# Moving cache copies, weight sums and a sigmoid inside one hybrid decoder layer

## The chip, the cores and the metric

The kernel runs on one core of a Trainium2 chip. TensorE (PE) multiplies matrices, VectorE (DVE), ScalarE (ACT) and GpSimd (POOL) work element by element, and SyncE (SP) and POOL issue the transfers. The metric is the device time of one execution in microseconds, the median over several runs.

## The reference

One layer for a prompt of 1024 rows and 32 sample rows (8 sequences of 4), model width 1024. All is float32.

```python
xn = RMSNorm_pre(x); h = xn @ w_in     # columns: q_attn | k_attn | v_attn | q_ret | k_ret | v_ret |
                                       #   ret_gate | merge_gate_attn | merge_gate_ret
# branch A: sliding-window (128) attention with sinks, 8 query heads, 2 key/value heads
# branch B: retention, 4 heads, key 128, value 256, in chunks of 128:
scores = einsum('bihd,bjhd->bhij', q, k) * dmask
out    = einsum('bhij,bjhe->bihe', scores, v) + cross ; state = g**L * state + k_decayed^T v
# each branch projected to 1024, merged by per-channel sigmoid gates, then w_o
x = x + RMSNorm_post(mixer)
x = x + RMSNorm_post(ConvFFN(RMSNorm_pre(x)))   # u = xn @ w_up, conv of width 3, gelu(a) * b, @ w_down
# also returned: the last 128 keys and values of the prompt, the caches of the samples
# (old rows shifted by 4, new rows behind), the retention states and the convolution states
```

What matters here: the sample caches are the old caches from row 4 on, copied as they are; the merge multiplies each branch by the sigmoid of its gate columns; and `w_down`'s product follows the feed-forward's middle.

## The kernel before

**Products.** Each float32 operand is split into two parts of reduced precision, `hi` (a cast on ACT, L228, L243, L246, L331) and `lo` (the difference, on DVE, L223). A product is three matmuls: `hi` with `xh`, `hi` with `xl`, `lo` with `xh` (L255, L256, L257, function `mm3`). The large products also use a scheme with seven products in place of eight (`A11`, `A12`, `A22`, `S1` to `S4`). The S products need sums of quarters of the weights. For `w_r` (the retention branch's projection) and `w_down` a "quad" of four quarters is loaded on SP (`quad_load`, two transfers of 256 KB, L289), four DVE operations on 128x256 make the sums (`quad_sums`, L223), and one store of 512 KB on POOL's queue puts them into DRAM (`r_d`, `s_d`, L300), from where the later stage loads them as weights (`quad_weights`, L316).

**Stages.** Normalisation and attention come first. Then `stream` runs the input projection of the retention and gate columns in pairs of 128 columns, and each pair's post function (`post_qk`, `post_gate`, `post_ga`, `post_gm`) stores it to DRAM: `qk_d`, `gr_d`, `a_d`, `gm_d`. The generator is advanced by `adv(n)`, so that its matmuls fill PE between the steps of the sample's and the prompt's retention. Of the prompt's retention, block `g` has three steps: `front` (scores, L1132), `middle` (output and state, L1152) and `tail` (gating). Tile `tt` of a head is one block of 128 rows. The `tail` of the first blocks of each head also issues one quad each: two of `w_r` and one of `w_down`, in tiles `zt`, which have three buffers and also serve `post_ga` (L849) and `z_sums`. After the retention comes the merge: the `w_r` product in the order of `PORD`, with `z_done` adding each product into `Gr`, and `merge`, which loads the gate `g_in` and the gated attention branch `a_in`, applies the sigmoid on ACT (L1257), and multiplies and adds on POOL for the first four column tiles (L1260, L1261) and on DVE for the others. `w_o` is loaded and split in the same loop (`weights`, L234). Raw weights of both, `w_raw`, share two buffers. Then follow the product with `w_o` (L1343), the feed-forward (24 pairs, each with `w_up` weights, convolution, gelu, and from `down_sums` one quad of `w_down`), and the down projection.

**Order.** The code's order is not the engines' order. A scheduler with a timeline of its own orders the instructions of each engine by their dependences. Instructions that are pinned keep their order among each other; the quads' loads and the cache copies are pinned. `ld` issues on SP's queue, `st` on POOL's, and each queue is in order: an issue that waits for a buffer holds all behind it.

Of the kernel before, what the change touches and what calls it, by code (L numbers as in the profile page):

```python
# [9 lines left out]
F32 = mybir.dt.float32  # L10
F32R = mybir.dt.float32r
U32 = mybir.dt.uint32
AF = mybir.ActivationFunctionType
# [5 lines left out]
P = 128  # L19
# [4 lines left out]
DB, DS = 8, 4  # L24
# [86 lines left out]
HW = T // 4  # L111
# [9 lines left out]
def trunk(ctx, tc, I, O):  # L121
    nc = tc.nc
    mult, add, sub = ALU.mult, ALU.add, ALU.subtract
    V, S, G, TE = nc.vector, nc.scalar, nc.gpsimd, nc.tensor
    ld, st = nc.sync, nc.gpsimd

    def pool(name, bufs=1, stack=None, side="right", **kw):
        if stack is not None:
            kw.update(side=side, reuse_waits="tile")
        return (stack or ctx).enter_context(tc.tile_pool(name=name, bufs=bufs, **kw))  # L130

    w_in, w_up, w_down = I["w_in"][0], I["w_up"][0], I["w_down"][0]
    w_o, w_a, w_r = I["w_o"][0], I["w_a_proj"][0], I["w_r_proj"][0]
# [8 lines left out]
    r_d = dram.tile([4, 1, P, KD, 2 * P], F32, name="r_d")  # L142
# [9 lines left out]
    s_d = dram.tile([4, 3, P, KD, 2 * P], F32, name="s_d")  # L152
# [21 lines left out]
    rt_stack, ph_stack, sm_stack = (ExitStack() for _ in range(3))  # L174
# [5 lines left out]
    def pin(ins):  # L180
        tc.keep_in_program_order(ins)
# [110 lines left out]
    def quad_sums(d, m, pt, kk, q, eng=None):  # L292
        eng = eng or V
        q = q[:, :, :2 * P]
        a11, a12, a21, a22 = (q[:, r::2, u * P:u * P + P] for u in range(2) for r in range(2))
        ew(eng, a22, a21, a22, add)
        ew(eng, a21, a11, a21, sub)
        ew(eng, a11, a22, a11, sub)
        ew(eng, a12, a12, a11, sub)
        st.dma_start(out=d[m, pt, :, 4 * kk:4 * kk + 4], in_=q)  # L300

    def down_sums(n, q):
        quad_load(w_down, n // 6, n // 2 % 3, n % 2, q)
        quad_sums(s_d, n // 6, n // 2 % 3, n % 2, q)
# [337 lines left out]
    for v in range(2):  # L642
        a, b = halves[v], halves[1 - v]
# [129 lines left out]
    def quarters(t):  # L773
        return t.rearrange("p (k x) -> p k x", k=4)
# [35 lines left out]
    def ST(name, shape, dt=F32, **kw):  # L810
        return rp.tile(list(shape), dt, name=name, **kw)

    def of_half(d, j):
        return d.rearrange("i p t -> p i t")[:, :, 2 * HW * j:2 * HW * (j + 1)]

    def both(t):
        return t.rearrange("p (i c) -> p i c", i=2)
# [34 lines left out]

    def post_gm(m):
        def post(j, o):
            st.dma_start(out=of_half(gm_d[KD + m:KD + m + 2], j), in_=both(o))
        return lambda j, o: lambda: post(j, o)

# [213 lines left out]
        for _ in sample(h):  # L1071
            adv(3)

    for nm in "kv":
        pin(st.dma_start(out=O[nm + "_sample"][0].rearrange("b r k d -> b r (k d)")[:, 0:P - DS, :],
                         in_=I["cache_" + nm][0].rearrange("b r k d -> b r (k d)")[:, DS:P, :]))

    ph_stack.close()
    wx["raw"] = rp = pool("rp", 1, stack=ph_stack)

# [18 lines left out]
    zlast, gts, qks, vts, state, quads, NBLK = [], {}, {}, {}, {}, {}, 4 * NB  # L1099
# [60 lines left out]
    def tail(g, pt, o):  # L1160
        h, tt = divmod(g, NB)
        tr_ = turn(pt, o)
        a = NS + P * tt
        while a < NS + P * tt + P:
            j = a // (2 * HW)
            b = min(NS + P * tt + P, 2 * HW * (j + 1))
            z = both(gts[h, j])[:, :, a - 2 * HW * j:b - 2 * HW * j]
            V.tensor_tensor(out=z, in0=tr_[:, :, a - NS - P * tt:b - NS - P * tt], in1=z, op=mult)
            a = b
        if tt == 0:  # L1170
            g_ = both(gts[h, 0])[:, :, 0:NS]
            V.tensor_tensor(out=g_, in0=g_, in1=z8[:, h], op=mult)
        QS = [(w_r, r_d, h, 0, 0), (w_r, r_d, h, 0, 1), (w_down, s_d, 3, (20 + h) // 2 % 3, h % 2)]
        if tt < 3:
            quads[h, tt] = quarters(ST("zt", (P, T), bufs=3))
            w, _, *at = QS[tt]
            quad_load(w, *at, quads[h, tt])
        if 0 < tt < 4:
            quad_sums(*QS[tt - 1][1:], quads.pop((h, tt - 1)))
        if tt in (4, NB - 1):  # L1180
            z_sums(h, gts[h, tt // 5], tt // 5)

# [36 lines left out]
    for g in range(NBLK):  # L1219
# [4 lines left out]
        m = middle(g, *f)  # L1224
# [14 lines left out]
    ps_stack.close()  # L1239
    tr = pool("tr", 1, stack=tr_stack)  # L1240
    wop = pool("wop", 1, stack=ph_stack)
    gpool = pool("apool", 2, stack=ph_stack)
    p8 = ppool("p8", 4, ps_stack)
    Gr = [TT("Gr%d" % m) for m in range(KD)]

# [6 lines left out]
    def merge(m, half):  # L1252

        ga = [gpool.tile([P, 2, HW], F32, name=q) for q in ("g_in", "a_in")]
        for t, d in zip(ga, (gm_d[KD + m], a_d[m])):
            ld.dma_start(out=t, in_=halves_of(d)[:, :, half])
        S.activation(ga[0], ga[0], AF.Sigmoid)  # L1257
        v = halves_of(Gr[m])[:, :, half]
        eng = G if m < 4 else V
        eng.tensor_tensor(out=v, in0=v, in1=ga[0], op=mult)  # L1260
        eng.tensor_tensor(out=v, in0=v, in1=ga[1], op=add)  # L1261
# [31 lines left out]
    for pi, p in enumerate(PORD):  # L1293
        first = p not in (A12, S3, S4)
        for c in range(2):
            hi, lo = wnext
            if 2 * pi + c + 1 < 2 * len(PORD):
                wnext = z_weights(2 * pi + c + 1)
            for e in range(2):
                for j in range(2):  # L1300
                    if first:
                        zb[c, e, j] = ps_8(j)[:, :HW]
                    ps = zb[c, e, j]
                    zh, zl = z_place(2 * pi + j)
                    for k in range(4):
                        mm3(ps, hi[:, 4 * e + k], lo[:, 4 * e + k], zh[:, k], zl[:, k],
                            first and k == 0, k == 3, skip_group_check=not first)
                    z_done(p, 2 * c + e, j, ps)
        for n in {0: (8, 9), 1: (10, 11), 3: (12, 13)}.get(pi, ()):
            load_zt(n)  # L1310
        if p == A22:
            merged_to_X(0)
        for m in {0: (0,), 1: (1,), 2: (2,), 3: (3, 4), 4: (5,), 5: (6,), 6: (7,)}.get(pi, ()):
            wo.append(weights(1, D, [(lambda r: r[:, 0], w_o[m * P:(m + 1) * P, :])],
                              [wop, wop, tpool, tpool, tpool, tpool, tpool, None][m]))
    merged_to_X(1)
# [11 lines left out]
    for tt in [0, 4, SMP, 1, 2, 3, 5, 6, 7]:  # L1328
# [4 lines left out]
        o = TT("o_t", (P, D))[:r_]  # L1333
# [20 lines left out]
        r = rsqrt_mean(s2[:, 0:1], D, r_, 1)  # L1354
# [8 lines left out]
        r = rsqrt_mean(s1, D, r_, 1)  # L1363
# [78 lines left out]
    for p in (A11, S1, A12, S4):  # L1442
        r, half = {A11: (0, 0), A12: (1, 0), S1: (0, 1), S4: (1, 1)}[p]
# [92 lines left out]
    for i in range(len(plain), NPAIR):  # L1536
        if i == NPAIR - 1:
            conv(i - 1, *done)
        u = pair(i)
        if i < NPAIR - 1:  # L1540
            prepare(i + 1)
            conv(i - 1, *done)
        if i < NPAIR - 2:
            down_sums(i - 2, tr.tile([P, 4, HW], F32, name="t2"))
        done = u
    def down_weights(p, c, pt):

# [186 lines left out]
```

## Time and profile before

| | |
|---|---|
| median of 3 runs | 1677.59 us (1676.19 to 1682.43) |
| the profiled execution | 1682.11 us, its span 1680.3 us |
| PE busy | 1633.0 us, 97% |
| DVE, ACT, POOL busy | 1207.2, 862.6, 434.8 us |
| granted TensorE clock, mean | 0.992 |

The span runs from the first to the last recorded instruction; 1.8 us lie around it. The profiled execution is 4.5 us slower than the median. Times in the traces count from the span's start. The line of PE's busy tenths in 40 slices of 42 us shows where PE had gaps:

```profile
PE   8999999999998999989999999999999999999997
```

A digit 9 stands for 90% or more. The slices below 9 are the first, the last, and two in between, from about 504 and 714 us on.

### The profile page before, as it was taken

What the parts mean: (1) busy time and instruction counts of PE and PEld (TensorE: products, weight loads), DVE (VectorE), ACT (ScalarE), POOL (GpSimd) and SP (SyncE); (2) the same over time, 40 slices, a digit from 0 to 9 for tenths busy, and PEclk for the clock granted to TensorE, in tenths of its full rate; (3) what the DMA queues carried; (4) which work ended last, traced back from release to release, by engine and by line L of the source; (5) the groups of instructions that cost most, each with busy time, mean ns of one, the idle gap of its engine ahead of it and who ended that gap; (6) DMA issues with size and microseconds to landing.
All of it is one profiled execution on the core that took longest, in us unless ns stands there. A gap on an engine that the chain in (4) does not pass through costs nothing.

```text
span 1680.3 us, 32489 instructions
## 1 busy us (share of the span) xinstructions
PE 1633.0 (97%) x12551; PEld 1593.2 (95%) x12551; DVE 1207.2 (72%) x2035; ACT 862.6 (51%) x1890; POOL 434.8 (26%) x654
## 2 busy tenths in 40 slices
PE   8999999999998999989999999999999999999997
PEld 7999989899998999989788999999999999999997
DVE  7887737688465566558757988888888888455476
ACT  6565634466564644454433655555555556443343
POOL 4242420012243333241312122222222223111111
PEclk9999999999999999999999999999999999999998
DMA  7212222565777686487722144444444447866664
GB/s 199 67 46 74 75 71 104 178 214 194 228 249 222 203 254 205 159 278 227 221 95 87 47 157 154 157 154 146 146 146 146 152 154 252 253 185 201 192 185 148
DMA packets 275852, 278.22 MB, mean 166 GB/s; under 512 B 23552, under 2 KB 234784, under 8 KB 275681
## 3 DMA queue, kind: packets, MB, share of 16 engines
q1 hardware_dynamic: 241937, 159.58, 32.6%
q0 software_dynamic: 33760, 116.57, 19.9%
q8 instruction: 98, 1.61, 0.4%
q14 instruction: 57, 0.47, 0.1%
HBM read 184.24 MB, written 87.49 MB: 162 GB/s over the span
## 4 chain that ended last, share of the span: by engine, by line
PE 78%; DMA 8%; DVE 5%; issue 4%; ACT 2%; POOL 1%; SPq 1%; DVEq 0%; POOLq 0%; ACTq 0%
PE ps_m L255 9%; PE ps_m L257 9%; PE ps_m L256 9%; PE ps_t L256 7%; PE ps_t L255 7%; PE ps_t L257 7%; PE ps_q L255 4%; PE ps_q L257 4%; PE ps_q L256 4%; PE ps_mm L255 3%; PE ps_mm L256 3%; PE ps_mm L257 3%; DMA qk<-qk_d 1%; DMA w_raw<-in_w_o 1%; DMA w_raw<-in_w_in 1%
## 5 line engine op out<-in xcount | busy, mean ns | idle before, releaser
L255 PE MATMUL ps_q<-xh,w 128*128 128x264 f32 x512 | 153.7, 300 | 7.5 <-DVE pair L939 6.2
L223 DVE SCALAR_TENSOR_TENSOR w_lo<-w_raw,w_hi 128x1024 fp32r<-128x1024 f32 x83 | 103.2, 1249 | 73.1 <-ACT w_hi L228 61.1
L257 PE MATMUL ps_m<-xh,w_lo 128*128 128x264 f32 x512 | 146.4, 286 | 4.6 <-DVE w_lo L223 4.5
L255 PE MATMUL ps_t<-xh,w_hi 128*128 128x264 f32 (+2 forms) x524 | 149.5, 285 | 0.0
L256 PE MATMUL ps_t<-xl,w_hi 128*128 128x264 f32 (+2 forms) x524 | 149.2, 285 | 0.0
L257 PE MATMUL ps_t<-xh,w_lo 128*128 128x264 f32 (+2 forms) x524 | 148.5, 283 | 0.0
L256 PE MATMUL ps_q<-xl,w 128*128 128x264 f32 x512 | 147.7, 289 | 0.0
L255 PE MATMUL ps_m<-xh,w_hi 128*128 128x264 f32 x512 | 146.4, 286 | 0.0
L257 PE MATMUL ps_q<-xh,w 128*128 128x264 f32 x512 | 146.3, 287 | 0.0
L256 PE MATMUL ps_m<-xl,w_hi 128*128 128x264 f32 x512 | 146.0, 285 | 0.0
L223 DVE SCALAR_TENSOR_TENSOR w<-w_raw,w 128x512 fp32r<-128x512 f32 x152 | 103.7, 686 | 32.6 <-ACT w L331 31.4
L1484 DVE SCALAR_TENSOR_TENSOR c_out<-u_ext,fconst,c_out 128x1024 f32<-128x1024 f32 x96 | 121.9, 1281 | 2.6 <-ACT c_out L1480 0.5
L228 ACT CAST w_hi<-w_raw 128x1024 fp32r<-128x1024 f32 x62 | 65.2, 1052 | 103.8 <-PE ps_t L256 75.4
L331 ACT CAST w<-w_raw 128x512 fp32r<-128x512 f32 x152 | 94.0, 621 | 24.9 <-DVE w_raw L223 11.1
L255 PEld LDWEIGHTS ps_q<-xh,w 128*128 128x128 f32 x512 | 97.9, 191 | 9.0 <-DVE pair L939 6.9
L257 PEld LDWEIGHTS ps_m<-xh,w_lo 128*128 128x128 f32 x512 | 96.8, 189 | 5.3 <-DVE w_lo L223 5.3
L255 PEld LDWEIGHTS ps_t<-xh,w_hi 128*128 128x128 f32 x524 | 99.1, 189 | 0.1
L257 PEld LDWEIGHTS ps_t<-xh,w_lo 128*128 128x128 f32 x524 | 99.2, 189 | 0.0
L256 PEld LDWEIGHTS ps_t<-xl,w_hi 128*128 128x128 f32 x524 | 99.1, 189 | 0.0
L256 PEld LDWEIGHTS ps_q<-xl,w 128*128 128x128 f32 x512 | 97.9, 191 | 0.5
L257 PEld LDWEIGHTS ps_q<-xh,w 128*128 128x128 f32 x512 | 97.6, 191 | 0.1
L255 PEld LDWEIGHTS ps_m<-xh,w_hi 128*128 128x128 f32 x512 | 96.8, 189 | 0.0
(446 smaller groups left out, 6000.6 us busy)
## 6 DMA issues: line engine op xcount, KB each, us to landing
w_raw<-in_w_up SPq DMA_DIRECT2D x48, 512.0 KB, 4.3
w_raw<-in_w_in SPq DMA_DIRECT2D x42, 512.0 KB, 4.5
w_raw<-s_d SPq DMA_DIRECT2D x60, 256.0 KB, 4.2
t_d<-t POOLq DMA_DIRECT2D x24, 528.0 KB, 4.0
t<-t_d POOLq DMA_DIRECT2D x24, 528.0 KB, 4.9
t<-in_w_down SPq DMA_DIRECT2D x40, 256.0 KB, 4.5
s_d<-t POOLq DMA_DIRECT2D x20, 512.0 KB, 3.6
w_raw<-in_w_down SPq DMA_DIRECT2D x36, 256.0 KB, 4.9
```

Of the source, the lines that this page charges most:

```text
L223: pinned(V.scalar_tensor_tensor(out=out, in0=in0, scalar=1.0, in1=in1, op0=mult, op1=op))
L228: pinned(S.copy(out=hi, in_=src))
L255: TE.matmul(ps, wh, xh, start=start, stop=False, **kw)
L256: TE.matmul(ps, wh, xl, start=False, stop=False, **kw)
L257: TE.matmul(ps, wl, xh, start=False, stop=stop, **kw)
L331: S.copy(out=t[:, 0:4], in_=src)
L1484: V.scalar_tensor_tensor(out=c[:, NS:], in0=u[:, g, NU + t:NU + t + SEQ], scalar=sc[t], in1=c[:, NS:], op0=mult, op1=add)
```

## The change

Four edits:

1. The copies of the old cache rows to the outputs (496 KB each for keys and values, from DRAM to DRAM, issued on POOL's queue) are no longer between the sample's and the prompt's retention, pinned. They are written in the feed-forward's loop, at pairs 4 and 6, and not pinned.
2. The four quads of `w_down` of the retention's `tail` (numbers 20 to 23) move to the feed-forward's loop, at pairs 5, 9, 13 and 17, each behind that pair's own quad and through the same single buffer `t2`. The `w_r` quads are now at blocks 0 and 2 of a head.
3. The sigmoid of the merge gate leaves `merge` (16 operations on 128x528) for `post_gm` (8 on 128x1056), ahead of the store to `gm_d`.
4. `g_in` and `a_in` have three buffers each in place of two, and the `w_o` tiles 5, 6 and 7 are asked for at products 4, 4 and 5 in place of 4, 5 and 6.

```diff
@@ -852,6 +852,7 @@
 
     def post_gm(m):
         def post(j, o):
+            S.activation(o, o, AF.Sigmoid)
             st.dma_start(out=of_half(gm_d[KD + m:KD + m + 2], j), in_=both(o))
         return lambda j, o: lambda: post(j, o)
 
@@ -1071,10 +1072,6 @@
         for _ in sample(h):
             adv(3)
 
-    for nm in "kv":
-        pin(st.dma_start(out=O[nm + "_sample"][0].rearrange("b r k d -> b r (k d)")[:, 0:P - DS, :],
-                         in_=I["cache_" + nm][0].rearrange("b r k d -> b r (k d)")[:, DS:P, :]))
-
     ph_stack.close()
     wx["raw"] = rp = pool("rp", 1, stack=ph_stack)
 
@@ -1170,13 +1167,13 @@
         if tt == 0:
             g_ = both(gts[h, 0])[:, :, 0:NS]
             V.tensor_tensor(out=g_, in0=g_, in1=z8[:, h], op=mult)
-        QS = [(w_r, r_d, h, 0, 0), (w_r, r_d, h, 0, 1), (w_down, s_d, 3, (20 + h) // 2 % 3, h % 2)]
-        if tt < 3:
+        QS = [(w_r, r_d, h, 0, 0), (w_r, r_d, h, 0, 1)]
+        if tt in (0, 2):
             quads[h, tt] = quarters(ST("zt", (P, T), bufs=3))
-            w, _, *at = QS[tt]
+            w, _, *at = QS[tt // 2]
             quad_load(w, *at, quads[h, tt])
-        if 0 < tt < 4:
-            quad_sums(*QS[tt - 1][1:], quads.pop((h, tt - 1)))
+        if tt in (1, 3):
+            quad_sums(*QS[(tt - 1) // 2][1:], quads.pop((h, tt - 1)))
         if tt in (4, NB - 1):
             z_sums(h, gts[h, tt // 5], tt // 5)
 
@@ -1239,7 +1236,7 @@
     ps_stack.close()
     tr = pool("tr", 1, stack=tr_stack)
     wop = pool("wop", 1, stack=ph_stack)
-    gpool = pool("apool", 2, stack=ph_stack)
+    gpool = pool("apool", 3, stack=ph_stack)
     p8 = ppool("p8", 4, ps_stack)
     Gr = [TT("Gr%d" % m) for m in range(KD)]
 
@@ -1254,7 +1251,6 @@
         ga = [gpool.tile([P, 2, HW], F32, name=q) for q in ("g_in", "a_in")]
         for t, d in zip(ga, (gm_d[KD + m], a_d[m])):
             ld.dma_start(out=t, in_=halves_of(d)[:, :, half])
-        S.activation(ga[0], ga[0], AF.Sigmoid)
         v = halves_of(Gr[m])[:, :, half]
         eng = G if m < 4 else V
         eng.tensor_tensor(out=v, in0=v, in1=ga[0], op=mult)
@@ -1310,7 +1306,7 @@
             load_zt(n)
         if p == A22:
             merged_to_X(0)
-        for m in {0: (0,), 1: (1,), 2: (2,), 3: (3, 4), 4: (5,), 5: (6,), 6: (7,)}.get(pi, ()):
+        for m in {0: (0,), 1: (1,), 2: (2,), 3: (3, 4), 4: (5, 6), 5: (7,)}.get(pi, ()):
             wo.append(weights(1, D, [(lambda r: r[:, 0], w_o[m * P:(m + 1) * P, :])],
                               [wop, wop, tpool, tpool, tpool, tpool, tpool, None][m]))
     merged_to_X(1)
@@ -1540,8 +1536,14 @@
         if i < NPAIR - 1:
             prepare(i + 1)
             conv(i - 1, *done)
+        if i in (4, 6):
+            nm = "kv"[i // 2 - 2]
+            st.dma_start(out=O[nm + "_sample"][0].rearrange("b r k d -> b r (k d)")[:, 0:P - DS, :],
+                         in_=I["cache_" + nm][0].rearrange("b r k d -> b r (k d)")[:, DS:P, :])
         if i < NPAIR - 2:
             down_sums(i - 2, tr.tile([P, 4, HW], F32, name="t2"))
+        if i in (5, 9, 13, 17):
+            down_sums(20 + (i - 5) // 4, tr.tile([P, 4, HW], F32, name="t2"))
         done = u
     def down_weights(p, c, pt):
```

What this does to the order is shown at four places; names are tiles with their buffer's number, DMA rows have the form of one transfer.

POOL, where the prompt's retention starts, before: the copies, then the loads of the first v tiles (`vt`) and the masks.

```order
L1060 DMA out_ret_sample<-s0_5263 128x2x256
L995 TENSOR_TENSOR rs_5473<-ms_5471,mhalf_107 32x1
L1075 DMA out_k_sample<-in_cache_k 8x15872
L1075 DMA out_v_sample<-in_cache_v 8x15872
L1113 DMA vt_5493<-v_d_64 128x256
L1113 DMA vt_5495<-v_d_64 128x256
L1113 DMA vt_5497<-v_d_64 128x256
```

The same place after:

```order
L1061 DMA out_ret_sample<-s0_5263 128x2x256
L996 TENSOR_TENSOR rs_5473<-ms_5471,mhalf_107 32x1
L1110 DMA vt_5491<-v_d_64 128x256
L1110 DMA vt_5493<-v_d_64 128x256
L1110 DMA vt_5495<-v_d_64 128x256
L1114 DMA dm_5497<-in_dmask 128x128
```

The copies are gone from there. POOL at the program's start, before:

```order
masks.py:197 MEMSET ident_102 128x128
L214 MEMSET mhalf_107 128x16
L521 MEMSET qs8_134 128x256
masks.py:199 ISA
masks.py:199 AFFINE_SELECT ident_102<-ident_102 128x128
L585 MEMSET acos_147 128x1056
L586 MEMSET asin_148 128x1056
```

and after:

```order
masks.py:197 MEMSET ident_102 128x128
L214 MEMSET mhalf_107 128x16
L521 MEMSET qs8_134 128x256
L1541 DMA out_k_sample<-in_cache_k 8x15872
masks.py:199 ISA
masks.py:199 AFFINE_SELECT ident_102<-ident_102 128x128
L1541 DMA out_v_sample<-in_cache_v 8x15872
L585 MEMSET acos_147 128x1056
L586 MEMSET asin_148 128x1056
```

The copies now stand behind the first memsets, at the very start, and not among the feed-forward's instructions.

SP around the quads of the second head, before (`z` and `zt<-gm_d` are gates, `qk` retention tiles, `w_raw` the stream's weights):

```order
L289 DMA zt_6475<-in_w_r_proj 128x4x128 x2
L849 DMA zt_6525<-gm_d_57 128x2x528
L289 DMA zt_6574<-in_w_r_proj 128x4x128 x2
L873 DMA w_raw_6598<-in_w_in 128x8x128
L1106 DMA qk_6497<-qk_d_62 128x2x128
L1122 DMA z_6611<-gr_d_63 128x2x528
L289 DMA zt_6672<-in_w_down 128x4x128 x2
```

and after:

```order
L289 DMA zt_6465<-in_w_r_proj 128x4x128 x2
L849 DMA zt_6515<-gm_d_57 128x2x528
L874 DMA w_raw_6585<-in_w_in 128x8x128
L1103 DMA qk_6487<-qk_d_62 128x2x128
L1119 DMA z_6598<-gr_d_63 128x2x528
L289 DMA zt_6659<-in_w_r_proj 128x4x128 x2
L874 DMA w_raw_6823<-in_w_in 128x8x128
```

The `w_down` quad is gone and the second `w_r` quad stands three loads later, behind the next `w_raw`, a `qk` and a `z`.

SP in the merge, from the first S1 weights (`r_d`) on, before:

```order
L316 DMA w_raw_9545<-r_d_60 128x4x128 x2
L234 DMA w_raw_9654<-in_w_o 128x1024
L316 DMA w_raw_9660<-r_d_60 128x4x128 x2
L1256 DMA g_in_9580<-gm_d_57 128x2x264
L316 DMA w_raw_9737<-r_d_60 128x4x128 x2
L1256 DMA a_in_9581<-a_d_58 128x2x264
L1256 DMA g_in_9615<-gm_d_57 128x2x264
L234 DMA w_raw_9814<-in_w_o 128x1024
L1256 DMA a_in_9616<-a_d_58 128x2x264
L1256 DMA g_in_9695<-gm_d_57 128x2x264
L316 DMA w_raw_9820<-r_d_60 128x4x128 x2
```

and after:

```order
L316 DMA w_raw_9513<-r_d_60 128x4x128 x2
L234 DMA w_raw_9620<-in_w_o 128x1024
L1253 DMA g_in_9582<-gm_d_57 128x2x264
L1253 DMA g_in_9667<-gm_d_57 128x2x264
L234 DMA w_raw_9626<-in_w_o 128x1024
L1253 DMA a_in_9583<-a_d_58 128x2x264
L1253 DMA a_in_9668<-a_d_58 128x2x264
L316 DMA w_raw_9632<-r_d_60 128x4x128 x2
```

A second `w_o` load stands ahead of the second S1 tile (`w_raw_9632`). The end of that stretch after:

```order
L234 DMA w_raw_9782<-in_w_o 128x1024
L1253 DMA g_in_9853<-gm_d_57 128x2x264
L1253 DMA a_in_9854<-a_d_58 128x2x264
L1253 DMA g_in_9885<-gm_d_57 128x2x264
L1253 DMA a_in_9886<-a_d_58 128x2x264
L1253 DMA g_in_9917<-gm_d_57 128x2x264
L316 DMA w_raw_9788<-r_d_60 128x4x128 x2
L1253 DMA a_in_9918<-a_d_58 128x2x264
```

The second tile of S4 (`w_raw_9788`) now stands behind the gate load `g_in_9917`, where its counterpart `w_raw_9820` stood ahead of most of the last gates.

## The prediction

> **What bounds the kernel now.** I read the busy shares first, then the span cut by stage, then the waits of PE, and last the 40 us around each wait.
>
> ```profile
> PE 1633.0 (97%) x12551; PEld 1593.2 (95%) x12551; DVE 1207.2 (72%) x2035; ACT 862.6 (51%) x1890; POOL 434.8 (26%) x654
> 320.00:700.00 380.00, 366.66 (x2823) 358.84 (x2822) 243.57 (x498) 205.01 (x522) 116.43 (x182) 0.98 0.67 212
> 925.00:1410.00 485.00, 485.00 (x3993) 485.00 (x3992) 423.61 (x698) 279.78 (x573) 128.34 (x214) 1.00 0.45 146
> ```
>
> The first line is the page's; the others are stretches: length, then busy us of PE, weight loads, DVE, ACT and POOL, the granted clock, the DMA share and GB/s. PE is the bound: busy for 1633.0 us, and in the feed-forward stage (925 to 1410) for all of 485. No matmul is added or removed, so time can only come from PE's idle gaps and from slow clock, and both lie ahead of 840 us, in the projection and retention (320 to 700), the merge, and the start of the product with w_o behind it.
>
> ```profile
> PE ps_q L255 <- DVE pair L939: 6.2, 3, 5.0
> PE ps_m L257 <- DVE w_lo L223: 4.5, 2, 4.3
> PE ps_m L1343 <- DVE o_t L1357: 3.1, 1, 3.1
> PE ps_a L1132 <- DMA qk<-qk_d: 2.7, 1, 2.7
> 440.00:480.00 40.00, 37.26 (x265) 36.15 (x264) 17.94 (x39) 19.63 (x49) 10.99 (x19) 0.91 0.78 237
> 520.00:560.00 40.00, 35.02 (x253) 33.94 (x253) 23.81 (x55) 18.88 (x46) 13.76 (x22) 0.91 0.77 241
> 720.00:760.00 40.00, 35.68 (x280) 35.34 (x279) 25.18 (x19) 22.53 (x37) 18.66 (x16) 0.96 0.90 295
> 800.00:840.00 40.00, 36.95 (x197) 30.05 (x195) 28.19 (x48) 17.13 (x39) 16.30 (x13) 1.00 0.73 220
> ```
>
> The waits give the total, the count and the longest, in us. Each of the four longest lies alone in one of the stretches below it: qk in 440:480, the pair sum in 520:560, w_lo in 720:760, o_t in 800:840. A stretch with a granted clock of 0.91 lost another 40 x 0.09 = 3.6 us, the one at 0.96 lost 1.6, the last none. So the four places cost 2.7 + 3.6, 5.0 + 3.6, 4.3 + 1.6 and 3.1: 23.9 us, the most that this change can win there. Each edit touches one of them.
>
> **1. The cache copies.**
>
> ```profile
> 438.20 0.57 POOL L1075 DMA_DIRECT2D out_k_sample<-in_cache_k  x1
> out_v_sample<-in_cache_v POOLq DMA_DIRECT2D x1, 496.0 KB, 7.2
> 439.47 10.91 DMA qk<-qk_d
> w_raw<-in_w_in SPq DMA_DIRECT2D x42, 512.0 KB, 4.5
> qk<-qk_d SPq DMA_DIRECT2D x32, 128.0 KB, 3.7
> ```
>
> The timeline's and the chain's rows have start and duration, the DMA rows the size and the median time to landing. The first qk tile is issued on SP right behind a w_raw load, 1.3 us after the first copy, and lands 10.91 us later, where 3.7 is usual. A w_raw load usually takes 4.5; with qk behind it in the same queue I expect qk, without the copies, at 444 to 446 (439.47 plus 4.5, and up to 2 for its own bytes). PE stood from 447.7 to 450.4. In the changed order the first qk product stands behind 14 fewer matmuls, and at 37.26 / 265 = 0.14 us each it is asked for at about 445.7. So nearly all of 2.7 + 3.6 goes: -6.0 (ends -6.3 and 0, if w_raw and the v tiles held qk up, not the copies).
>
> The copies don't go where the code puts them. Nothing holds them to the feed-forward loop, and in the order of the changed kernel they stand on POOL at the very start, behind a handful of memsets. The feed-forward pays nothing, the start does:
>
> ```profile
> 0.92 0.31 POOL L521 MEMSET qs<- 128x256 f32 x1
> 3.14 1.05 ACT L490 ACTIVATE xn<-xt 32x1024 f32<-32x1024 f32 x1 [1.12 <-DMA xt<-in_x_sample]
> 3.28 3.75 PE L517 MATMUL ps_mm<-g_row,one 1*128 1x512 f32 x4 [3.28 <-DMA g_row<-in_g_pre_mix]
> 4.00:6.00 2.00, 2.00 (x4) 0.67 (x2) 0.72 (x2) 0.66 (x3) 0.54 (x1) 1.00 0.95 371
> 14.00:16.00 2.00, 1.42 (x4) 0.92 (x4) 2.00 (x4) 2.00 (x3) 0.00 (x0) 1.00 0.03 12
> ```
>
> Issued from 1.2 us on, behind that memset (0.92 + 0.31), they meet the first loads: PE and ACT wait for g_row and x until 3.2, and the DMA engines are full (0.95) just after, at 371 GB/s. At this rate 992 KB are 2.7 us. The loads that decide land by 3.3, when the copies have hardly begun, and by 14 the queue has run empty (0.03), which takes up the rest: I take +1.0, between 0 and 2.7 + 1.8 of slow clock. The issues (0.57 each) stand ahead of POOL's later work there and hide in its waiting.
>
> **2. The weight sums of the down projection.**
>
> ```profile
> 528.50 7.47 DMA r_d<-zt
> 536.46 6.25 DMA zt<-in_w_down
> 542.80 0.89 DVE L223 SCALAR_TENSOR_TENSOR zt<-zt 128x256 f32<-128x256 f32 x2 [6.93 <-DMA zt<-in_w_down]
> zt<-in_w_r_proj SPq DMA_DIRECT2D x16, 256.0 KB, 6.1
> ```
>
> Chain rows: the store of one quad frees its buffer at 535.97, the load of the w_down quad follows and lands at 542.71, and DVE stands 6.93 us before its sums, with the add that frees PE's bank behind them. With two quads a head the three buffers suffice and no load waits for a store. In the changed order the second w_r quad's load stands behind the next w_raw, a qk and a z; issued at about 530 and landing 6.1 later it is there at 536.1, where DVE arrives at 535.87 (542.80 less 6.93). I leave 1.0 of the 8.6: -7.6 (ends -8.6 and -3).
>
> What they cost in the feed-forward:
>
> ```profile
> L223 DVE SCALAR_TENSOR_TENSOR t<-t 128x256 f32<-128x256 f32 x80 | 33.5, 419 | 11.0 <-DMA t<-in_w_down 11.0
> 1040.00:1080.00 40.00, 40.00 (x331) 40.00 (x331) 33.45 (x57) 22.11 (x47) 9.13 (x16) 1.00 0.46 147
> t<-in_w_down SPq DMA_DIRECT2D x40, 256.0 KB, 4.5
> s_d<-t POOLq DMA_DIRECT2D x20, 512.0 KB, 3.6
> ```
>
> Four quads of four sums of 0.419 us are 6.7 us of DVE in 485, 1.7 us each time, and DVE has 6.5 idle us in 40. The 2 MB of loads and 2 MB of stores go over DMA engines that are 46% used. Cost 0; if the cover were gone, 6.7.
>
> **3. The sigmoid.**
>
> ```profile
> L1257 ACT ACTIVATE g_in<-g_in 128x528 f32<-128x528 f32 x16 | 10.2, 643 | 11.3 <-DMA g_in<-gm_d 10.9 <-DVE xl L223 0.3
> L843 ACT ACTIVATE pair<-pair 128x1056 f32<-128x1056 f32 x8 | 8.7, 1088 | 0.1
> 824.54 1.05 ACT L246 CAST w_hi<-w_raw 128x1024 fp32r<-128x1024 f32 x1 [7.55 <-DMA w_raw<-in_w_up]
> 825.49 0.64 ACT L1257 ACTIVATE g_in<-g_in 128x528 f32<-128x528 f32 x1
> 826.21 1.83 POOL L1260 TENSOR_TENSOR Gr<-Gr,g_in 128x528 f32<-128x528 f32 x1 [2.28 <-ACT g_in L1257]
> 830.58 0.60 ACT L1351 ACTIVATE o_t<-ps_m 128x512 f32<-128x512 f32 x1 [3.21 <-DVE xl L223]
> 739.07 1.23 DVE L223 SCALAR_TENSOR_TENSOR w_lo<-w_raw,w_hi 128x1024 fp32r<-128x1024 f32 x1 [0.55 <-ACT w_hi L228]
> 751.12 2.31 DVE L223 SCALAR_TENSOR_TENSOR w_lo<-w_raw,w_hi 128x1024 fp32r<-128x1024 f32 x1
> ```
>
> Sixteen of 0.643 go, eight of 1.088 (the like of L843's) come, where ACT is busy for 205 of 380 us: 0 to +2, taken +0.5 for bank evictions that stand behind them. At 824.5 the last sigmoid stands behind a cast that waited 7.55 us for a w_up tile; POOL's merge, DVE's split and ACT's o_t follow in that order, and PE waits 3.1. Without the sigmoid the merge waits for transfers and z products alone: -3.1 (ends -3.1 and 0). The 4.3 at w_lo are another thing: the same DVE form takes 2.31 us in place of 1.23 while POOL merges. The POOL work stays and only its times shift: -1.5 of 5.9 (ends -5.9 and +2).
>
> The Trainium skill's "SBUF — State Buffer", under "Who interferes with whom", says that a DVE operation with two SBUF inputs and a GpSimd operation that reads SBUF lock each other out for a whole instruction. The row of 2.31 agrees, and by this rule the 5.9 wouldn't fall at all.
>
> **4. Third buffer, w_o loads.** The raw weight tiles go round two buffers in SP's order. Before the second S1 tile there now stand two w_o loads where one stood, and the second S4 tile's load stands behind the last gates'.
>
> ```profile
> 779.12 3.67 DMA w_raw<-in_w_o
> 783.59 3.90 DMA w_raw<-r_d
> 788.68 0.66 DVE w_lo L223
> ```
>
> These are on the chain already, so there is no slack: one slot more is 783.59 - 779.12 = 4.5 us. In the changed order PE has w_o matmuls and the high products of several banks to do meanwhile. Taken +2.5, between 0 and 4.5 + 1.8 of slow clock.
>
> **Sum.** -6.0 + 1.0 - 7.6 + 0.5 - 3.1 - 1.5 + 2.5 = -14.2. The profiled execution took 1682.1 us, 4.5 over the median of 1677.6: so 1667.9. If that excess lies outside these places, the median comes to 1663.4; if it lies in them, to 1667.9. I take a third of it off: 1666, 11 to 12 us under the median of before.
>
> A rule would change the sum: "TensorE: Matmul & The Clock Gate" of the Trainium skill, under "What's actually happening", lets the clock fall after an idle window of about 3.4 us. By it the 2.7 us stall could cost no clock, and the sum would be 3.6 less: about 1670. The row of 0.91 at 440:480 says otherwise, the 1.00 after 3.1 idle us agrees, so I keep the row.
>
> **Rivals.** *New waits in the merge (0.15).* For it: term 4 lies on the chain, and a SP queue with more gate loads ahead of weights. Against: PE has other products in the order. At its end with a second such wait at S4, +7 instead of +2.5 and nothing won at w_lo: about 1672.
>
> *The start pays in full (0.12).* The copies hold g_row and x back: +4.5 for +1.0, about 1670, still inside the bound of 0.5%.
>
> *The DVE and POOL collision grows (0.08).* POOL's merges no longer wait for ACT, so they follow each other without a pause; w_lo operations double more often. +2 for -1.5, and half of the 3.1 stays: 1671. This is what the SBUF rule would make of it.
>
> *Slower (0.08): DVE stands in the feed-forward.* The added quads pass through one buffer: its store takes 3.6 us and the next load 4.5, so 8.1 from one quad's last sum to the other's first. Ten rows stand between them in DVE's order, at 33.45 / 57 = 0.59 us and 84% busy some 7 us. DVE would stand 1.1 us, which its 6.5 idle us cover; if the load comes late on SP's queue, 6 or more, with the adds that empty PE's banks behind it. From about 5 us on PE stops; four stops of 3.2 with 1.8 of slow clock are 20: 1686.
>
> **How the numbers follow.** The forecast has 0.57, with a range of its own of 1658 to 1669. About 0.5% (8.4 us) is what can be told from no change; faster means under 1669.2. The first three rivals end within it, but a few of their cases fall below: faster 0.60, same 0.32, slower 0.08. Low end: all of w_lo's 5.9, no new wait and the other two thirds of the 4.5: 1666 - 4.4 - 2.5 - 3.0 = 1656. High end: two of the rivals together, 1678.
>
> **What would show it.** qk landing before 447 and no PE wait at the first block of retention; two DMAs at 1 to 3 us on POOL, and the first PE instruction at 3.3 to 4.5; no DVE wait for zt over 2 us around 535; no PE wait for o_t after the merge; PE at 485 of 485 in the feed-forward. I am wrong if PE's waits for w_lo in the merge exceed 8 us together, if PE's start is later by over 3, or if the pair sum at 540 still waits for a zt load.

## The result, and the profile after

The changed kernel takes 1682.69 us (1677.58 to 1687.32), the kernel before 1676.32 us in the same comparison. The ratio is 1.0039, 95% interval 1.0028 to 1.0050: 6.5 us slower, where 10 to 12 us less were forecast. It is within the 0.5% that the prediction called no change, but clear of zero, on the other side, and above the 1678 that the prediction gave as its high end.

The profiled execution of the changed kernel took 1682.09 us, as much as the profiled one of the kernel before (1682.11). Against their medians the two stand differently: the one of before is 5.8 us above its median, the one of after is on it. So a second profile of the kernel before is needed beside the first; it comes below.

The page after, its busy times and PE's tenths:

```profile
PE 1633.1 (97%) x12551; PEld 1592.4 (95%) x12551; DVE 1207.4 (72%) x2035; ACT 863.2 (51%) x1882; POOL 428.8 (26%) x654
PE   7999999999999999999999999999999999999997
```

The two dents of before at 504 and 714 us are gone. The first slice has gone from 8 to 7. The waits of PE on which the reading rests (total, count, longest):

```profile
PE ps_a L461 <- DVE xn L494: 6.0, 2, 4.7
PE ps_b L1003 <- ACT o L997: 3.5, 2, 1.9
PE ps_a L1129 <- DVE state L1149: 3.3, 3, 2.3
PE ps_m L257 <- DVE w_lo L223: 2.8, 2, 2.2
PE ps_m L255 <- ACT u_ext L418: 2.0, 2, 1.3
PE ps_m L255 <- ACT w_hi L228: 1.6, 1, 1.6
PE ps_m L1339 <- DVE o_t L1353: 0.7, 1, 0.7
```

Lines stand a few lower than before. The waits for qk and for the pair sum at 540 are gone, the longest for w_lo is halved, o_t's is 0.7. In their place stand a wait of 4.7 at the start, longer waits for `state` and `o` (the retention's state and its output) than before, and new ones for `w_hi` in the merge and for `u_ext` (the feed-forward's products, as ACT writes them) in the feed-forward. By stretches, first before (the start), then after (the start and the feed-forward):

```profile
0.00:40.00 40.00, 33.55 (x190) 29.56 (x191) 28.87 (x54) 26.40 (x53) 16.39 (x29) 1.00 0.75 208
```

```profile
0.00:40.00 40.00, 28.67 (x159) 24.30 (x160) 27.06 (x45) 22.24 (x40) 16.03 (x28) 1.00 0.80 227
925.00:1410.00 485.00, 482.85 (x3969) 482.19 (x3969) 425.87 (x713) 277.67 (x571) 123.05 (x214) 1.00 0.48 153
```

PE does 4.9 us less in the first 40 us, and the feed-forward, full before, loses 2.2 us. The start after, in the timeline:

```profile
1.36 0.71 POOL L1541 DMA_DIRECT2D out_k_sample<-in_cache_k  x1
2.42 0.56 POOL L1541 DMA_DIRECT2D out_v_sample<-in_cache_v  x1
3.37 3.75 PE L517 MATMUL ps_mm<-g_row,one 1*128 1x512 f32 x4 [3.37 <-DMA g_row<-in_g_pre_mix]
10.17 1.06 ACT L490 ACTIVATE xn<-xt 128x1024 f32<-128x1024 f32 x1 [5.80 <-DMA xt<-in_x_prompt]
11.22 0.57 ACT L595 COPY g_pre<-ps_mm 128x512 f32<-128x512 f32 x1
12.20 2.74 PE L461 MATMUL ps_a<-ident,xn 32*128 32x32 f32 x12 [4.71 <-DVE xn L494]
```

and the two rows of it before:

```profile
5.63 1.06 ACT L490 ACTIVATE xn<-xt 128x1024 f32<-128x1024 f32 x1 [1.34 <-DMA xt<-in_x_prompt]
7.85 2.63 PE L461 MATMUL ps_a<-ident,xn 32*128 32x32 f32 x12 [0.45 <-DVE xn L494]
```

The copies are issued at 1.36 and 2.42 us, beside the first loads. The load that PE waits for first, g_row, is as early as before. The first prompt tile is not: ACT gets it at 10.17 in place of 5.63, its square is the first step to everything behind it, and PE stands from 7.5 to 12.2. The DMA engines were not full while it stood. The stretch from 8 to 9 us, first before, then after:

```profile
8.00:9.00 1.00, 0.97 (x7) 0.84 (x8) 1.00 (x2) 0.29 (x2) 0.00 (x0) 1.00 1.17 293
```

```profile
8.00:9.00 1.00, 0.00 (x0) 0.00 (x0) 0.00 (x0) 0.00 (x0) 0.00 (x0) 1.00 0.15 54
```

Their busy share (the last figure but one, summed from packet times) is 0.15 where it was 1.17. The tile is late, but not because the engines lacked bandwidth all that time; what held its data back is not shown.

### The profile page after: what moved, and what is told of

Same layout as the page of the kernel before. It is cut to its first block, busy times and chain, and to the rows that moved or that the text cites. A ratio compares the mean times of both kernels' runs of the same rounds, so it can differ in the third digit from the quotient of the medians.

```text
span 1680.3 us, 32499 instructions
## 1 busy us (share of the span) xinstructions
PE 1633.1 (97%) x12551; PEld 1592.4 (95%) x12551; DVE 1207.4 (72%) x2035; ACT 863.2 (51%) x1882; POOL 428.8 (26%) x654
## 4 chain that ended last, share of the span: by engine, by line
PE 75%; DMA 9%; DVE 9%; issue 3%; ACT 3%; SPq 1%; POOL 0%; DVEq 0%; ACTq 0%; POOLq 0%
PE ps_m L255 8%; PE ps_m L257 8%; PE ps_m L256 8%; PE ps_t L256 6%; PE ps_t L257 6%; PE ps_t L255 6%; PE ps_q L255 5%; PE ps_q L257 5%; PE ps_q L256 5%; PE ps_mm L255 2%; PE ps_mm L256 2%; PE ps_mm L257 2%; DMA zt<-in_w_r_proj 2%; DMA t<-in_w_down 2%; DMA w_raw<-in_w_o 1%
## 5 line engine op out<-in xcount | busy, mean ns | idle before, releaser
L255 PEld LDWEIGHTS ps_q<-xh,w 128*128 128x128 f32 x512 | 97.5, 190 | 3.1 <-ACT pair L917 1.5
L256 PEld LDWEIGHTS ps_m<-xl,w_hi 128*128 128x128 f32 x512 | 97.1, 190 | 0.1
```

The lines of the kernel that those rows point to most:

```text
L255: TE.matmul(ps, wh, xh, start=start, stop=False, **kw)
L256: TE.matmul(ps, wh, xl, start=False, stop=False, **kw)
```

## The experiments

Each is timed against the kernel before on the same chip; "ratio" is to that, with its 95% interval. Three dots in a diff stand for arguments that are the same.

**Where the copies stand.** Four kernels. `a_pin` is the changed kernel with the copies pinned in the feed-forward:

```diff
         if i in (4, 6):
             nm = "kv"[i // 2 - 2]
-            st.dma_start(...)
+            pin(st.dma_start(...))
```

> The changed kernel with its two cache copies pinned, so that POOL issues them in the feed-forward and not at the program's start. Theory 1 (the copies at the start are what the change lost): PE's wait of 4.7 us at 7.5 us and the later warm clock (23.1 for 19.8, 1.7 us) go, so some 6.4 us less than the changed kernel, 1676, and PE's shift against the kernel before is about 0 at 40 us. Rival (the other edits cost what they bring, and the start is made up by later slack): 1682, unchanged.

Measured: 1677.0 us, ratio 1.0002 (0.9994 to 1.0011). Six us less than the change, level with the kernel before. The copies' place makes the loss. The other edits, with the copies away from the retention, together bring nothing that can be told from zero.

`b_copy0` is the kernel before with the copies alone moved, not pinned:

```diff
-    for nm in "kv":
-        pin(st.dma_start(...))                # between the retentions
...
+        if i in (4, 6):
+            st.dma_start(...)                 # in the feed-forward's loop
```

> The kernel before with only the copies moved, unpinned as in the change, so that they stand at the program's start. Theory 1: +6.4 us at the start, and -6 where the first qk tile is no longer late: 1676 to 1677, the same as before. If the qk wait isn't the copies' doing, or a typical run of the kernel before doesn't have it: 1681 to 1683.

Measured: 1682.6 us, ratio 1.0045 (1.0032 to 1.0058). This edit alone is as slow as the whole change. The expected gain of 6 did not come. The time is in the range of the second case, but for neither of its reasons: the wait for qk is gone from this profile, and a second profile of the kernel before (below) has it.

`b_copyffn` is the same with `pin(...)` around the copies, so that POOL issues them in the feed-forward.

> The kernel before with only the copies moved, pinned in the feed-forward. Theory 1: the qk wait of 2.7 us and its slow clock of 3.4 go and nothing comes at the start: 1670. Rival (qk was late because of w_raw and the v tiles): the wait stays, 1676.

Measured: 1676.6 us, ratio 1.0003 (0.9993 to 1.0012). Both expectations missed: the qk wait is gone, and the time is the same. What PE waited for between 440 and 490 us, first in the kernel before (its second profile, below), then here:

```profile
PE ps_a L1133 <- DMA qk<-qk_d: 2.7, 1, 2.7
```

```profile
PE ps_a L1128 <- DVE state L1148: 1.5, 1, 1.5
PE ps_b L1002 <- ACT o L996: 1.4, 1, 1.4
```

2.7 us of waiting for a transfer became 2.9 us of waiting for the retention's own chain; that its DVE and ACT steps had run while PE waited for qk is the likely reason. This is not all of it: the clock of this stretch is better (1.00 in place of 0.96), and the table below shows that the kernel is ahead at 600 us and loses it again by 900.

`a_orig` is the changed kernel with the copies put back between the two retentions.

> The changed kernel with the copies put back to where the kernel before has them, the other edits kept. Theory 1: no start cost (-6.4), the qk wait is back (+6): about 1682, and what the other edits bring is to be read as this run less the kernel before. If the other edits bring the 14 us that the prediction's terms gave them less the new waits, 1670; if they bring nothing, 1676.

Measured: 1676.3 us, ratio 0.9999 (0.9989 to 1.0010). The other three edits together bring nothing that can be told from zero.

**A second profile of the kernel before** (`before2`, unchanged but for a comment line, so its lines stand one higher).

> The kernel before, unchanged, for a second profile of it. The first profiled execution took 1682.1 us, and the median of the runs is now 1676.2. If the four waits (qk 2.7, pair sum 5.0, w_lo 4.3, o_t 3.1, with 8.5 us of slow clock) belong to every execution, they stand here again with the same lengths, within 0.5 us, at a time near 1682. If the profiled execution had an unlucky clock, the waits are there and most of the 8.5 us of slow clock isn't: 1674 to 1678. If the waits themselves vary, two or more of the four are shorter by over 1 us.

Measured: 1675.5 us. Its waits, and the stretches with the granted clock (the last but two):

```profile
PE ps_m L258 <- DVE w_lo L224: 5.4, 2, 4.8
PE ps_q L256 <- DVE pair L940: 3.9, 2, 3.7
PE ps_m L1344 <- DVE o_t L1358: 0.6, 1, 0.6
```

```profile
440.00:480.00 40.00, 37.25 (x272) 36.01 (x271) 19.81 (x43) 19.99 (x51) 10.16 (x18) 0.96 0.85 258
520.00:560.00 40.00, 36.28 (x265) 34.95 (x263) 23.36 (x53) 19.17 (x48) 12.78 (x21) 0.96 0.76 238
720.00:760.00 40.00, 35.22 (x277) 35.00 (x276) 27.88 (x26) 24.12 (x42) 20.98 (x16) 0.96 0.89 281
```

The qk wait is the same to the tenth. The pair sum's is 3.7 in place of 5.0, o_t's 0.6 in place of 3.1, and the two stretches at 0.91 are at 0.96: 1.6 us of slow clock where the first profile had 3.6. So the four places hold 2.7 + 1.6, 3.7 + 1.6, 4.8 + 1.6 and 0.6: 16.6 us in this execution, 23.9 in the first.

With two profiles of the kernel before, progress can be compared. All traces have 12551 matmuls, so the table counts them: how much later (+) or earlier the matmul starts that this second profile starts at the given time. Each row is one execution.

| | 40 us | 300 us | 600 us | 900 us | 1450 us |
|---|---|---|---|---|---|
| the change | +5.0 | +6.1 | +2.5 | +3.7 | +6.6 |
| `b_copy0` | +4.1 | +5.2 | +5.2 | +10.8 | +10.8 |
| `b_k0` (next) | +1.7 | +2.8 | +4.5 | +3.5 | +3.5 |
| `b_copyffn` | +0.1 | +0.2 | -4.0 | -0.5 | -0.5 |
| `b_quads` (below) | -0.4 | -0.4 | -1.5 | -1.3 | -1.2 |

The change loses 5 us at the start, gains 3.6 between 300 and 600 us, and loses 1.2 up to 900 us and 2.8 in the feed-forward. `b_copyffn` is 4 us ahead at 600 us; waits between 610 and 840 us and the slow clock behind them take it back, and what makes these was not tried.

**How much copy at the start.** `b_k0` has the key copy at the start, the value copy pinned in the feed-forward.

```diff
+        if i == 4:
+            st.dma_start(... "k" ...)
+        if i == 6:
+            pin(st.dma_start(... "v" ...))
```

> The kernel before with the key copy alone at the program's start and the value copy pinned in the feed-forward. With both at the start the time was 6 us more than with both in the feed-forward. Theory 1 (the copies' bytes stand in the way of the first prompt tile's load, and ACT waits for that tile in its order, with the gate row's copy behind it): half the bytes, so x lands some 2.3 us late in place of 4.5, PE's wait grows by 2.3, and the time is 1678 to 1680. Rival (the first copy alone holds the engines until the tile is late, or it is a fixed cost of any copy there): 1682. Rival (the first copy hides and the second does the harm): 1676.

Measured: 1680.5 us, ratio 1.0025 (1.0014 to 1.0035), between the rivals, nearest to theory 1. The row that answers:

```profile
9.00 1.06 ACT L490 ACTIVATE xn<-xt 128x1024 f32<-128x1024 f32 x1 [2.47 <-DMA xt<-in_x_prompt]
```

Here the first tile is in time and the second is late, 9.00 where the kernel before has it by 7.2. By the ratios one copy costs 4.2 us (2.3 to 5.9), two cost 7.5 (5.4 to 9.7); by the table PE is 1.7 and 4.1 to 5.0 us behind at 40 us. By both, one copy costs less than two; its harm is to the second tile.

`a_attn` is the changed kernel with the copies pinned in the attention, behind the first loop over its blocks.

> The changed kernel with its copies pinned in the attention, some 100 us from the start, where the DMA engines are 22% busy. Theory 1: no cost there, as in the feed-forward: 1676 to 1677. If the copies in the feed-forward had a part in its new waits for u_ext (2.9 us in the changed kernel): 1674.

Measured: 1674.3 us, ratio 0.9995 (0.9983 to 1.0007). So all three places away from the start that were tried (here, the feed-forward, between the retentions) give the time of the kernel before, within noise.

**The other edits one by one.** `b_quads` moves only the weight sums of the down projection.

> The kernel before with only the four weight sums of the down projection moved. Theory 1 (the wait at 540 shrinks by 2 to 3 us and some clock, and the feed-forward gains waits for u_ext of 2 to 3): 1675 to 1677, with PE under 485.0 of 485 in the feed-forward. By the prediction's terms (7.6 gained, feed-forward free): 1668. If the new waits in the feed-forward belong to another edit, PE has 485.0 of 485 there.

Measured: 1673.7 us, ratio 0.9983 (0.9970 to 0.9995): 2.9 us gained. Its feed-forward:

```profile
925.00:1410.00 485.00, 484.96 (x3991) 484.75 (x3990) 426.76 (x715) 278.83 (x568) 121.24 (x215) 1.00 0.49 158
```

Alone the sums are free there. At 536 us PE's wait for the pair sum is replaced by one of 2.4 for `state`. The chain to it, a row of the chain and two of the timeline:

```profile
528.03 9.21 DMA zt<-in_w_r_proj
537.37 0.89 DVE L223 SCALAR_TENSOR_TENSOR zt<-zt 128x256 f32<-128x256 f32 x2 [3.97 <-DMA zt<-in_w_r_proj]
538.64 0.49 PE L1132 MATMUL ps_a<-qk 128*128 128x128 f32 x2 [2.44 <-DVE state L1152]
```

DVE still stands for a quad: now for the second `w_r` quad, which takes 9.2 us to land. `state` follows these sums in DVE's order, at 538.17, and PE waits for it.

`b_sig` moves only the sigmoid.

> The kernel before with only the sigmoid moved to the products' output. The second profile of the kernel before has the wait for w_lo (4.8 us) and none for o_t. Theory A (in a usual execution the sigmoid is on no path): 1675 to 1677, the same, w_lo's wait within 1 us of 4.8, no wait for o_t. Theory B (the sigmoid sets POOL's merges, and these double DVE's splits): w_lo's wait falls by 2 to 3 us, 1673. If the sigmoids delay evictions in the projection: new waits for ACT between 600 and 720 us, 1678.

Measured: 1679.3 us, ratio 1.0008 (0.9995 to 1.0021), no difference that can be told. Waits from 700 to 840 us:

```profile
PE ps_m L257 <- DVE w_lo L223: 2.5, 3, 1.0
PE ps_m L256 <- DVE w_loT L223: 2.5, 1, 2.5
PE ps_q L255 <- DVE pair L942: 1.8, 1, 1.8
PE ps_m L255 <- ACT w_hi L228: 1.1, 1, 1.1
```

By the ratio theory A has the time, though the median is above its range; theory B has the fall of w_lo's wait (5.4 to 2.5), and neither the new wait for the split of a w_o tile, w_loT, which takes most of it back. The rows of that wait:

```profile
812.14 3.69 POOL L1261 TENSOR_TENSOR Gr<-Gr,a_in 128x528 f32<-128x528 f32 x2 [1.38 <-DMA a_in<-a_d]
812.35 2.32 DVE L223 SCALAR_TENSOR_TENSOR w_loT<-w_raw,w_hiT 128x1024 fp32r<-128x1024 f32 x1
814.72 0.50 PE L256 MATMUL ps_m<-w_loT,xh 128*128 128x512 f32 x1 [2.46 <-DVE w_loT L223]
```

The split takes 2.32 us beside POOL's merges; the median of this form in the trace is 1.23.

`b_bufwo` has only the third gate buffer and the earlier w_o loads.

> The kernel before with only the third buffer for the gates and the earlier w_o loads. Theory A (the two w_o loads ahead of the S1 weights make the new wait for w_hi at 781 to 787 us of 1.6 to 2.3 that the kernels with all edits show): that wait is here, and the time is 1677 to 1680. Rival (the wait for w_hi comes with the other edits' order): no wait for w_hi over 1 us, and w_lo's wait falls by the earlier gate loads: 1673 to 1676.

Measured: 1680.0 us, ratio 1.0023 (1.0011 to 1.0035): 3.9 us lost, with the wait where it was expected. PE's waits from 760 to 800 us, then rows of the timeline:

```profile
PE ps_m L255 <- ACT w_hi L228: 3.5, 2, 2.9
```

```profile
777.86 0.35 SPq L234 DMA_DIRECT2D w_raw<-in_w_o  x1
778.48 0.52 SPq L1256 DMA_DIRECT2D a_in<-a_d  x1
779.10 0.56 SPq L1256 DMA_DIRECT2D g_in<-gm_d  x1
780.39 0.52 SPq L1256 DMA_DIRECT2D a_in<-a_d  x1
781.53 1.86 SPq L316 DMA_DIRECT2D w_raw<-r_d  x2
787.61 1.04 ACT L228 CAST w_hi<-w_raw 128x1024 fp32r<-128x1024 f32 x1 [1.79 <-DMA w_raw<-r_d]
```

SP issues the second w_o tile, three gate loads, and only then the S1 weights; ACT gets these at 787.6.

Then what was still open, the halves of this edit: `b_wo` has the w_o loads alone, `b_buf` the buffer alone.

> The kernel before with the earlier w_o loads alone, two gate buffers. If two w_o tiles ahead of the second S1 weights make the wait for w_hi (2.9 us with both halves of the edit): the wait stands here near 786 us and the time is 1679 to 1681. If the third gate buffer makes it, by gate loads ahead of weights on SP: no wait for w_hi over 1 us, 1676.

> The kernel before with the third gate buffer alone, w_o loads as before. If the w_o loads make the wait for w_hi: none here, 1676 or, by earlier gate loads for the merges, 1674. If the buffer makes it: the wait near 786 and 1679 to 1681.

Measured: 1676.1 us, ratio 0.9996 (0.9983 to 1.0009), and 1675.1 us, ratio 1.0000 (0.9986 to 1.0014). Neither half makes the wait; the longest for w_hi is 0.8 and 0.9 us. By these runs it takes both, the second w_o tile and the gate loads that the third buffer lets through, ahead of the weights.

**Without the losing parts.** `c_qa`: weight sums moved and copies pinned in the attention, the rest as before. `c_qas`: with the sigmoid moved too.

> The kernel before with the weight sums moved and the copies pinned in the attention; sigmoid, buffers and w_o loads as before. The weight sums alone gave -2.9 us. Theory A (taking the qk wait away only uncovers the next waits of the retention's chain, as with the copies alone in the feed-forward): 1673 to 1674, with new waits for o and state between 455 and 485 us. Theory B (the two add up): 1669 to 1671.

> As the run with weight sums and copies in the attention, and the sigmoid moved as well; buffers and w_o loads as before. If the sigmoid is on no path, the same as that run within 1.5 us, without a wait for w_hi near 780. If the new waits for u_ext in the feed-forward (1.2 to 2.9 us in the kernels with all edits, none with the weight sums alone) come with the sigmoid's move, they stand here: +2. If they come with the buffers and w_o loads, PE has 485.0 of 485 here.

Measured: 1673.1 us, ratio 0.9979 (0.9964 to 0.9994), and 1674.1 us, ratio 0.9978 (0.9970 to 0.9987). With the sums alone at 0.9983, the copies' move adds nothing that can be told, as theory A of `c_qa` had it. Both have waits for u_ext in the feed-forward again, so neither the sigmoid nor the third buffer is needed for them; nor is the copies' move, as `a_orig`, with the copies in their old place, has 483.76 of 485. For `c_qas`, the feed-forward and SP's wait in it:

```profile
925.00:1410.00 485.00, 483.52 (x3975) 482.96 (x3974) 424.41 (x710) 276.27 (x564) 125.02 (x216) 1.00 0.50 161
```

```profile
SPq L289 <- DMA s_d<-t: 92.9, 13, 12.7
```

SP stands 92.9 us in all, each time until the store of one quad has landed, with w_up's loads queued behind. The same wait stands in `b_quads`, where PE lost nothing:

```profile
SPq L289 <- DMA s_d<-t: 91.6, 13, 12.6
```

So the wait alone does not stop PE. `c_t01` sends the extra quads through t0 and t1 in turn:

```diff
         if i in (5, 9, 13, 17):
-            down_sums(20 + (i - 5) // 4, tr.tile([P, 4, HW], F32, name="t2"))
+            down_sums(20 + (i - 5) // 4, tr.tile([P, 4, HW], F32, name="t%d" % ((i - 5) // 4 % 2)))
```

> As the run with weight sums, sigmoid and copies in the attention (1674.1 us, 0.9978 of the kernel before, PE 483.5 of 485 in the feed-forward), but the four extra quads go through the buffers t0 and t1 in turn, not through t2 behind that pair's own quad. Theory A (the store of the first quad holds the second's load on SP, and w_up's loads behind it): SP's wait for s_d<-t of 92 us falls to under 30, PE has 485.0 of 485, 1 to 2 us less. Theory B (t0 and t1 serve the convolution, so the load waits for that in the same way): SP's wait moves to other names, and PE's waits stay.

Measured: 1671.5 us, ratio 0.9972 (0.9960 to 0.9984), the lowest median of all: 4.7 us under the kernel before, 11 under the change. Its interval overlaps those of `c_qas` and `c_qa`, so the 1 to 2 us that were expected between them cannot be told.

```profile
925.00:1410.00 485.00, 485.00 (x3992) 485.00 (x3992) 426.49 (x711) 277.34 (x565) 130.33 (x216) 1.00 0.51 161
```

```profile
SPq L289 <- DMA s_d<-t: 6.6, 2, 4.1
```

Theory A has SP's side, a wait of 6.6 in place of 92.9. PE is full, as it should be by theory A, but it is so in `b_quads` too. `c_q2` has two extra quads in place of four, the other two at pairs 22 and 23:

```diff
-        if i < NPAIR - 2:
-            down_sums(i - 2, tr.tile([P, 4, HW], F32, name="t2"))
-        if i in (5, 9, 13, 17):
-            down_sums(20 + (i - 5) // 4, ...)
+        down_sums(i - 2, tr.tile([P, 4, HW], F32, name="t2"))
+        if i in (9, 17):
+            down_sums(22 + (i - 9) // 8, ...)
```

> As the run with weight sums, sigmoid and copies in the attention, but two of the four extra quads at pairs 22 and 23, which had none, so only two pairs have two quads. Theory A: SP's wait for s_d<-t halves to some 45 us and PE's loss in the feed-forward to under 1 us: 1673. If the waits are chance of the order: PE's loss anywhere between 0 and 2.5.

Measured: 1678.5 us, ratio 1.0017 (1.0002 to 1.0033), a miss. SP's wait halved as expected, to 48 us, but PE has 482.3 of 485: it now waits 1.8 us at 1396, and 2.3 more for the down projection's first weights at 1423. The late sums at pairs 22 and 23 may make both; that was not tried.

## Why the prediction was wrong

Two kinds of step failed. The gains that were booked for waits of one profile, -17.7 us together, measured -1.1 in the single edits (+0.5, -2.9 and +1.3, each uncertain by some 2 us). And the cost of the start, the one loss that turned no gain into 6.5 us lost, was taken too low, by the wrong load. That the change would come out slower had 0.08, for a stop of DVE in the feed-forward; the feed-forward lost 2.2 to 2.8, the start 5.0.

*The start, +1.0 taken, at most 4.5.* It measured +7.5 us (ratio 1.0045, 5.4 to 9.7; 6.0 between the medians of copies at the start and in the feed-forward; 4.1 to 5.0 of it at 40 us). That the copies stand at the start was read rightly from the order. The failed sentence is that only the loads landing by 3.3 us decide. The prompt tile of 5.63 decides: 4.5 us late, PE's wait grew by 4.3. The rest was taken to hide because the DMA queue had run empty by 14 us; a late first tile isn't made good by an empty queue later. "The start pays in full" had 0.12 and +4.5; the direction was right, and 992 KB at the full rate (2.7 us) was not an upper end: the tile lost 4.5. The sign that the prediction named, PE's first instruction at 3.3 to 4.5 us, came (3.37) and told nothing, as that instruction waits for g_row and not for the tile.

*The copies out of the retention, -6.0.* The wait ended as forecast, and the time stayed (1.0003). The step left out is what is late next: on the spot `o` and `state`, 2.9 us for 2.7, and further on waits between 610 and 840 us, which took back the 4.0 us that the kernel was ahead at 600. The first is shown; why the later ones grew stays open. The slow clock counted on it, 3.6 us, was 1.6 in the second profile.

*The weight sums, -7.6.* It measured -2.9 (-0.8 to -5.0). Of the 8.6 us taken from the first profile, 5.3 were there in the second. The step that failed is the landing of the second `w_r` quad: taken at 6.1 us behind its issue, it took 9.2 in `b_quads`, and in the changed kernel DVE stood 3.6 us for it. The load that holds DVE changed its name, `state` stands behind it, and PE waits 2.4 for that. *Their cost in the feed-forward, 0:* right for the sums alone (484.96 of 485), not with other edits beside them (482.85 to 483.76). The cover was counted in DVE's idle time. The queue to ask was SP's, which stands over 90 us for the one buffer in all of these: the slower rival named the buffer, the 8.1 us from sum to sum and a late load on SP, and laid the stop on DVE at a price of 20; the traces have 0 to 2 us of PE. That two buffers in turn end SP's wait is shown; why PE loses in some of these orders and not in `b_quads` is open.

*The sigmoid, -4.1 with the merge.* Measured 1.0008, so between 0.8 us gained and 3.5 lost. Its main term, o_t, was mis-sized: 3.1 in the first profile, 0.6 in the second, and 0 to 2.0 in the other kernels with the sigmoid in the merge. With the sigmoid moved the same row is at most 0.7, but two of these kernels wait 1.5 and 2.1 for o_t at a later product, so whether the wait went or only moved is open. What took the rest back is the wait of 2.5 for w_loT, whose split took 1.1 us longer than its usual 1.23 beside POOL's merges. The lock between DVE and POOL that the Trainium skill's "SBUF — State Buffer" describes under "Who interferes with whom" agrees with this row. No run here takes POOL's merges away, so it is not shown to be the reason.

*Buffers and w_o loads, +2.5.* Right in kind, with 3.9 measured (1.8 to 5.9, the range taken was 0 to 6.3). But the single slot of 4.5 us was not the reason: the w_o loads alone cost nothing that can be told.

*The base.* The sum was made against one execution that stood at the top of its kernel's runs, and a third of the 4.5 us was taken off. The second profile has 16.6 of the 23.9 us, so 7.3 of them did not belong to every execution.

The single edits add up to 7.5 - 2.9 + 1.3 + 3.9 = 9.8 us with some 2 us of uncertainty each; the whole change has 6.5 (4.7 to 8.4).

## What to carry to other kernels

A transfer that depends on nothing is placed by the scheduler, not by the line it is written in: look where it stands in its queue, and pin it. At a program's start, ask which loads the first long chain needs in turn, not which one is waited for first. Before a wait is booked as a gain, ask of a second profile whether it is there again, and of the chain behind it what will be late next.

## What was not expected of the hardware

Two copies of 496 KB between places in DRAM delayed a 512 KB load, issued 0.2 us after the first of them, from 5.63 to 10.17 us, more than their bytes at the rate of 371 GB/s (2.7 us). Each copy went as 8 packets of 63,488 bytes of 2.3 to 2.5 us, the first copy's from 3.4 us on, the second's from 6.3 to 9.3. The engines' busy share was 0.15 from 8 to 9 us, so it was not the rate that held the load to the end; the cause is open. One copy alone left the first tile in time and delayed the second, from 7.2 to 9.0 us.

The same wait of 2.7 us for qk cost 3.6 us of slow clock in one execution and 1.6 in the next, and with the waits of 1.4 and 1.5 in its place none:

```profile
440.00:480.00 40.00, 37.85 (x289) 36.48 (x288) 20.50 (x44) 20.32 (x52) 11.45 (x19) 1.00 0.88 267
```

The six other kernels that keep the copies there waited 2.4 to 3.1 us for qk: five have the stretch at 0.96, and `b_buf`, with a wait of 2.5, at 1.00. So in these runs the clock's price of a wait of this length is 0, 1.6 or 3.6 us, and a share of it has to be taken, not the one value that a profile shows. The Trainium skill's "TensorE: Matmul & The Clock Gate" says under "What's actually happening" that the windows run free of the program. That the price changes from one execution to the next agrees with it. The same section lets the clock fall after an idle window of about 3.4 us; a fall after a wait of 2.7 does not agree with that.
